# Hybrid encoder block on one core: attention's values behind the last forward output, a keys' piece and a queries' split at other places, the first output loads in one row

## The chip, the cores and the metric

The kernel runs on one core of a Trainium2 chip. The metric is the device time of one execution in microseconds (us), as the median of three runs; lower is better. A profiled execution is a separate one. The engines are TensorE (PE, with its weight loads PEld), VectorE (DVE), ScalarE (ACT), GpSimd (POOL) and SyncE (SP, which here issues DMAs only); ACT and POOL issue some DMAs too. Each engine works through its own instructions in a fixed order.

## What is computed

One layer of a bidirectional encoder with two branches, in float32:

```python
h = concat(meta_tokens, x)                       # 16 + 1024 = 1040 positions, D_MODEL = 1024
u = rms_norm(h) ; z = u @ w_in                   # one projection, split in ten parts:
rq, rk, rv, rg, aq, ak, av, ag, gr, ga = split(z)

# branch A: retention, 4 heads (dk 128, dv 256), chunks of 128, forward and backward
s     = (q k^T) * decay ;  inner = s v
state = chunk_decay * state + (k * k_decay)^T v        # scan over the chunks
o_r   = inner + (q * q_decay) state                    # both directions summed
y_r   = (group_norm(o_r) * ret_nw * silu(rg)) @ w_rb

# branch B: attention, 8 query heads, 2 key/value groups (hd 128), window +-128
aq, ak = rotary(aq), rotary(ak)
p   = softmax over [band of 3 x 128 keys | 16 meta keys | sink logit]
o_a = p[band] av + p[meta] av_meta
y_a = (o_a * silu(ag)) @ w_ab

mix = sigmoid(gr) * y_r + sigmoid(ga) * y_a
out = h + rms_norm(mix @ w_out, post_w)          # meta rows dropped
```

## The kernel before

**Precision and tiling.** Each fp32 product is made of three matmuls on upper and lower halves of the operands (`mm3`, L76 to L78). The upper half is a rounding cast on ACT or POOL, the lower half is value minus upper half on DVE (`dve_lo`, L92). So an operand is ready for PE only when ACT and then DVE are through with it. Tiles have 128 partitions; PSUM has eight banks, in four groups `pj` (3), `p1` (2), `p2` (2) and `p3` (1).

**Stages, in order of time.** Setup and retention of four heads; attention in 32 chunks of a head pair and 128 queries; then four phases of large projections, z (gates), r and a (the branches' projections) and o (the output). Each phase is a fast scheme of seven block products in place of eight: sums and differences of blocks of the left operand (tiles `st..S` such as sto1S, made on DVE at L1029) and of the right operand (T1 to T4, prepared early and fetched from DRAM by `get_pre`).

**Order.** A scheduler places the instructions of each engine by simulated times, within what the code demands: `follow(x)` and `tc.issue_after(x)` put what is issued inside behind instruction x on its engine. `latest` holds the last matmul, `last` named instructions, `marks` those of them that exist.

**Around the last head.** In retention `stage2` (L545) makes the forward output pa of a chunk in the one bank of `p3`: two `mm3`, then a scaled copy on ACT and an add on DVE (L557). Backward outputs pb_8 to pb_1 follow in a loop, each added on DVE (L645), transposed by PE (to, L621) and scaled on ACT (ost, L626). `gen_av` (L919) makes attention's values in nine pieces pav, the meta rows first; it is drawn from at three points behind the retention, the first without a condition, the second behind the last backward output.

**Attention.** For each chunk `stage1` makes scores ps, reduces them on DVE (L1467), takes exponentials on ACT (L1470), the reciprocal of their sum (L1474), and scales on POOL (L1483). `stage2` transposes p on PE (L1503 to L1508) and splits it in halves; `stage3` multiplies by the values (po). In between, `fill` draws projections of later queries and keys. The table `BEGUN` hooks work to steps of this fill: `keys(g, i)` splits the rotated keys of group g, piece i, in halves (kTh on ACT L742, kTl on DVE), `split_q(hp, e, i)` splits queries of head pair hp (aqh on ACT L695, aql on DVE). The rotation is two accumulating DMAs on POOL's queue (L192) behind two products on DVE (L187, L188).

**Loads of the phases.** `run` walks through all jobs (unit u, product p) and calls hooks at fixed steps. For phase o the raw blocks wro of units 0 and 1 are loaded 11 and 10 jobs before the phase (`o_load`, 512 KB each, from mx_d, which the branches have written); `refill("a", ...)` fetches T1 at -11 jobs, as a pair of transfers of 1 MB into both halves of big. u3a and u2a are sums in phase a, to which DVE adds a bank of PSUM (L1097); such a bank is free for PE's next product when it has been read.

Of the kernel before, what the change touches and what calls it, by code (L numbers as in the profile page):

```python
# [10 lines left out]
ALU = mybir.AluOpType  # L11
# [10 lines left out]
SCALE = 128 ** -0.5  # L22
# [17 lines left out]
def block_kernel(ctx: ExitStack, tc: tile.TileContext, x0, xT, x, meta, w_in, w_rb, w_ab, w_out, post_w,  # L40
# [50 lines left out]
    def dve_lo(o, i, hi):  # L91
        return nc.vector.tensor_tensor(o, i, hi.bitcast(F32), ALU.subtract).ins  # L92
# [377 lines left out]
    def retention(h, fill, begin=lambda: None):  # L470
# [11 lines left out]
        def qs(ts, c):  # L482
            return ts[(c - 1) // 4][:, P * ((c - 1) % 4):P * ((c - 1) % 4) + P]
# [64 lines left out]
        def stage2(c):  # L548
            n, vh, vl, kd, s = st1.pop(c)
            if c > 0:  # L550
                fh, fl = state["fs"]
                pa = p3(f"pa{h}_{c}")
                mm3(pa[:, 0:256], s[0], s[1], vh, vl, True, True)
                mm3(pa[:, 256:512], qs(qh, c), qs(ql, c), fh, fl, True, True)
                o = op[c - 1]
                nc.scalar.activation(o, pa[:, 0:256], AF.Copy, scale=rcol[:, c:c + 1])
                nc.vector.scalar_tensor_tensor(o, pa[:, 256:512], qdf(h, c), o, op0=ALU.mult, op1=ALU.add)  # L557
            if kd:
                pk = p2(f"pkv{h}_{c}")
            if "f" in kd:  # L560
                if c:
                    mm3(pk[:, 0:256], *kd["f"], vh, vl, True, True)
                else:
                    latest[:] = [nc.tensor.matmul(pk[:, 0:256], km, vm, start=True, stop=True).ins]
                new = rp.tile([P, 256], F32, tag="S", bufs=2, name=f"Sf{h}_{c}")
                if c == 0:
                    nc.vector.tensor_copy(new, pk[:, 0:256])
                else:
                    nc.vector.scalar_tensor_tensor(new, state["f"], cdf(h), pk[:, 0:256], op0=ALU.mult, op1=ALU.add)
                state["f"] = new  # L570
                state["fs"] = split_state(new, f"f{h}_{c}")
            if "b" in kd:
                a, b = kd["b"]
                mm3(pk[:, 256:512], a, b, vh, vl, True, True)
                nc.scalar.copy(kvb[c - 1], pk[:, 256:512])
# [154 lines left out]
    kT = {}  # L730
    wak = []

    rotated_k = {}

    def keys(g, i):

        if not i:
            kT[g] = [ra.tile([P, 4, 272], R, tag="kp", bufs=2, name=f"kT{s}{g}") for s in "hl"]
        kh, kl = kT[g]
        o = rotated_k.pop((g, i))  # L740
        s = NM if i == 0 else 0
        nc.scalar.copy(kh[:, i, 0:256], o[:, s:s + 256])  # L742
        dve_lo(kl[:, i, 0:256], o[:, s:s + 256], kh[:, i, 0:256])
        if i == 0:
            for j in range(4):
                nc.scalar.copy(kh[:, j, 256:272], o[:, 0:NM])
                dve_lo(kl[:, j, 256:272], o[:, 0:NM], kh[:, j, 256:272])
# [141 lines left out]
    def marks(*names):  # L889
        return [last[m] for m in names if m in last]  # L890
# [51 lines left out]


    av = gen_av()
    next(av)
    with follow(last["pb"]):
        next(av)
    with follow(*latest):
# [225 lines left out]
    def refill(nm, src):  # L1174
# [20 lines left out]
        def got(n):  # L1195
            return lambda: get_pre(n)

        def step(at, n, f):
            for k, j in enumerate(n):
                at.setdefault(j, []).append(lambda k=k: f(k))  # L1200
# [7 lines left out]
        if nm == "a":  # L1208
            at = {-16: [load(0, 0)], -14: [load(1, 1)]}
            each(at, -13, behind(split("B11", 0, 0)))  # L1210
            at.update({-11: [got("T1")], -10: [load(1, 0)], -9: [got("T2")], -5: [got("T3")], -1: [got("T4")]})
            each(at, -7, behind(split("B21", 1, 0)))
            each(at, -3, behind(split("B22", 1, 1)))
            return at
# [17 lines left out]
    def run(phases):  # L1232

        jobs = [(ph, u, p) for ph, _ in phases for u, p in ph.seq]
        hooks, i = {}, 0
        for ph, src in phases:
            i += len(ph.seq)
            if src:
                for j, f in refill(ph.nm, src).items():
                    hooks.setdefault(i + j, []).extend(f)  # L1240

        for u in (0, 1):
            hooks.setdefault(len(jobs) - len(ph_o.seq) - 11 + u, []).insert(0, lambda u=u: ph_o.block(u, "A11"))
        for k, at in enumerate((16, 27, 46, 58)):
            hooks[at] = [lambda k=k: pre_load(k, act_src(w_out))]
            for i in range(4):
                hooks[at + 4 + 2 * i] = [lambda k=k, i=i: pre_split(k, i, near[0])]
        n = 0
        for i, (ph, u, p) in enumerate(jobs):
            while n < min(i + LEAD, len(jobs)):  # L1250
                q, u_, p_ = jobs[n]
                q.prepare(u_, p_)
                n += 1
            yield
            ph.product(u, p)
            for f in hooks.get(i, ()):
                f()
# [83 lines left out]
        nc.vector.tensor_scalar(pw, pw, 0.5, None, op0=mul)  # L1341

    def o_load(t, u, j):
        nc.sync.dma_start(t, mx_d[4 * j:4 * j + 4, :, 256 * (u ^ 2):256 * (u ^ 2) + 256].rearrange("k p t -> p k t"))

    def o_post(u, i, j, o, to=None):
        if not rows:
# [82 lines left out]
    def attention():  # L1430
# [14 lines left out]
        def stage1(hp, n):  # L1445
# [10 lines left out]
            for x_ in range(2):  # L1456
# [7 lines left out]
                for c in ({0: (272, 336), 7: (208,)} if x_ else {0: (0,)}).get(n, ()):  # L1464
                    nc.vector.tensor_copy(r[:, c:c + 1], nsink[:, hp:hp + 1])
                o, w0 = (0, 64) if x_ else (1, 1)
                nc.vector.tensor_tensor_reduce(r[:, o:o + wid], s[:, 0:wid], seen, -SCALE,  # L1467
                                               nsink[:, hp:hp + 1], ALU.add, ALU.min, nm_[:, x_:x_ + 1])

                last["exp"] = nc.scalar.activation(pp[:, x_, w0 - o:w0 - o + 1 + wid], r[:, 0:1 + wid], AF.Exp,  # L1470
                                                   scale=-1.0, bias=nm_[:, x_:x_ + 1],
                                                   accum_out=den[:, x_:x_ + 1]).ins
                sides.append((wid, w0, blocks, moff))
            last["sum"] = nc.vector.reciprocal(den, den).ins  # L1474
            softmax.append(last["sum"])
            both = ap.tile([P, 2, 2, NM], F32, tag="pm2", bufs=2, name=f"pm2_{hp}_{n}")
# [86 lines left out]
        for k, (hp, n) in enumerate(chunks):  # L1563
# [15 lines left out]
            if not k:  # L1579
                with follow(*latest):  # L1580
                    fill(FILL[hp][n] - 5)
            with follow(*latest, *marks("exp", "sum")) if not ends else ExitStack():
                stage2(hp, n)
            if not ends:
# [7 lines left out]
            if k in (12, 14, 21):  # L1592
# [13 lines left out]
             76: [(sum_row, 3, 1)], 79: [(sum_fetch, 4)], 82: [(split_q, 2, 0, 0)], 88: [(sum_row, 4, 0)],  # L1606
             89: [(sum_row, 4, 1)], 90: [(split_q, 2, 1, 0)], 92: [(sum_fetch, 5)], 100: [(sum_row, 5, 0)],
             101: [(sum_row, 5, 1)], 102: [(fetch_aq, 3)], 104: [(keys, 1, 1)], 105: [(sum_fetch, 6)],
             110: [(split_q, 2, 0, 1)], 117: [(half_w, 'q', 3, 0)], 121: [(half_w, 'q', 3, 1)],
             122: [(pre_fetch, 9), (keys, 1, 2)], 123: [(sum_row, 6, 0)], 124: [(sum_row, 6, 1)], 126: [(split_q, 2, 1, 1)],  # L1610
             127: [(sum_fetch, 7)], 133: [(pre_sum, 9, 0)], 134: [(pre_sum, 9, 1)], 136: [(keys, 1, 3)],
             139: [(pre_sum, 9, 2)], 140: [(pre_parts, 9)], 141: [(pre_fetch, 10)], 145: [(split_q, 3, 0, 0)],
             146: [(sum_row, 7, 0)], 147: [(sum_row, 7, 1)], 150: [(split_q, 3, 1, 0)], 152: [(pre_sum, 10, 0)],
             153: [(pre_sum, 10, 1)], 155: [(pre_sum, 10, 2)], 157: [(pre_parts, 10)], 158: [(pre_fetch, 11)],
             164: [(split_q, 3, 0, 1)], 166: [(pre_sum, 11, 0)], 167: [(pre_sum, 11, 1)], 168: [(pre_sum, 11, 2)],
             170: [(pre_parts, 11)], 171: [(pre_fetch, 12), (split_q, 3, 1, 1)], 176: [(pre_sum, 12, 0)],
             178: [(pre_sum, 12, 1)], 179: [(pre_sum, 12, 2)], 181: [(pre_parts, 12)], 182: [(pre_fetch, 13)],
             187: [(pre_sum, 13, 0)], 188: [(pre_sum, 13, 1)], 189: [(pre_sum, 13, 2)], 190: [(pre_parts, 13)]}

# [112 lines left out]
```

## Time and profile before

| What | us |
|---|---|
| three runs | 1035.59, 1036.95, 1035.52 |
| their median | 1035.59 |
| profiled execution | 1040.78 |
| its span in the trace | 1039.0 |
| PE busy | 1023.5 |
| DVE busy | 834.6 |
| ACT busy | 505.2 |
| POOL busy | 230.1 |

Span is from the first to the last instruction of the trace. Rows of a timeline have the start in us from the span's start, the duration in us, engine, line, operation, output and inputs, shapes and count; in brackets the idle time of the engine just before, and what ended it. Matmuls overlap, so the next one starts before the listed duration is over. SPq, ACTq and POOLq are the sequencers that issue DMAs. The clock column is the granted clock of TensorE as a share of full speed.

### The profile page before, as it was taken

What the parts mean: (1) busy time and instruction counts of PE and PEld (TensorE: products, weight loads), DVE (VectorE), ACT (ScalarE), POOL (GpSimd) and SP (SyncE); (2) the same over time, 40 slices, a digit from 0 to 9 for tenths busy, and PEclk for the clock granted to TensorE, in tenths of its full rate; (3) what the DMA queues carried; (4) which work ended last, traced back from release to release, by engine and by line L of the source; (5) the groups of instructions that cost most, each with busy time, mean ns of one, the idle gap of its engine ahead of it and who ended that gap; (6) DMA issues with size and microseconds to landing.
All of it is one profiled execution on the core that took longest, in us unless ns stands there. A gap on an engine that the chain in (4) does not pass through costs nothing. (4 is left out here: it accounts for less than half of the span.)

```text
span 1039.0 us, 17320 instructions
## 1 busy us (share of the span) xinstructions
PE 1023.5 (99%) x5875; PEld 900.3 (87%) x5875; DVE 834.6 (80%) x1804; ACT 505.2 (49%) x1137; POOL 230.1 (22%) x368
## 2 busy tenths in 40 slices
PE   9999999999999999999999999999999999999997
PEld 8999999989998888988888888888888888887886
DVE  7787858769866778777769999998999899767765
ACT  5532332523423566655667555455567356243442
POOL 3445244243442323443310000000000000111042
PEclk9999999999999999999999999999999999999999
DMA  9433123242331457675559589898864846889463
GB/s 355 166 87 87 62 48 86 81 101 89 96 74 62 103 173 208 171 192 150 154 170 345 189 279 338 309 317 309 281 257 155 268 165 215 249 203 334 123 122 81
DMA packets 98840, 188.45 MB, mean 181 GB/s; under 512 B 13024, under 2 KB 37632, under 8 KB 98192
## 3 DMA queue, kind: packets, MB, share of 16 engines
q1 hardware_dynamic: 81200, 162.89, 46.4%
q0 software_dynamic: 10176, 14.73, 9.5%
q10 hardware_dynamic: 7376, 9.73, 2.8%
q8 instruction: 46, 0.75, 0.3%
q14 instruction: 42, 0.34, 0.1%
HBM read 124.32 MB, written 57.68 MB: 175 GB/s over the span
## 5 line engine op out<-in xcount | busy, mean ns | idle before, releaser
L1330 POOL DMA_DIRECT2D mx_d<-c1a x4 | 3.6, 892 | 395.1 <-DMA a<-in_w_out_dram 367.2
L77 PE MATMUL bz<-big,llz 128*128 128x512 f32 x192 | 74.8, 390 | 0.2 <-DVE llz L92 0.2
L78 PE MATMUL bz<-big,lhz 128*128 128x512 f32 x192 | 74.4, 389 | 0.0
L76 PE MATMUL bz<-big,lhz 128*128 128x512 f32 x192 | 74.1, 389 | 0.0
L76 PE MATMUL pv<-wh,big 128*128 128x256 f32 x256 | 72.9, 285 | 0.0
L78 PE MATMUL pv<-wl,big 128*128 128x256 f32 x256 | 72.6, 284 | 0.0
L77 PE MATMUL pv<-wh,big 128*128 128x256 f32 x256 | 72.2, 282 | 0.0
L77 PE MATMUL bz<-T,llz 128*128 128x512 f32 x176 | 68.5, 389 | 0.0
L78 PE MATMUL bz<-T,lhz 128*128 128x512 f32 x176 | 68.5, 389 | 0.0
L76 PE MATMUL bz<-T,lhz 128*128 128x512 f32 x176 | 68.1, 389 | 0.0
L1470 ACT ACTIVATE p<-raw,nm 128x337 f32<-128x337 f32 (+1 forms) x64 | 35.5, 556 | 36.5 <-DVE nm L1467 33.8
L1483 POOL TENSOR_SCALAR p<-p,den 128x336 f32<-128x336 f32 (+2 forms) x60 | 32.6, 566 | 87.9 <-DVE den L1474 87.8
L76 PE MATMUL paq<-big,wh 128*128 128x512 f32 x128 | 51.9, 406 | 0.0
L77 PE MATMUL paq<-big,wl 128*128 128x512 f32 x128 | 50.5, 394 | 0.0
L78 PE MATMUL paq<-big,wh 128*128 128x512 f32 x128 | 50.4, 394 | 0.0
L76 PEld LDWEIGHTS pv<-wh,big 128*128 128x128 f32 x256 | 48.4, 189 | 0.2
L77 PEld LDWEIGHTS pv<-wh,big 128*128 128x128 f32 x256 | 48.3, 189 | 0.0
L78 PEld LDWEIGHTS pv<-wl,big 128*128 128x128 f32 x256 | 48.2, 188 | 0.0
L77 PEld LDWEIGHTS bz<-big,llz 128*128 128x128 f32 x192 | 36.0, 188 | 8.0 <-DVE llz L92 0.5
L626 ACT ACTIVATE ost<-to,rnw 128x128 f32<-128x128 f32 x64 | 19.9, 366 | 46.6 <-PE to L621 36.2
L76 PEld LDWEIGHTS bz<-big,lhz 128*128 128x128 f32 x192 | 36.0, 188 | 7.4
L78 PEld LDWEIGHTS bz<-big,lhz 128*128 128x128 f32 x192 | 36.0, 188 | 7.4
(627 smaller groups left out, 3617.4 us busy)
## 6 DMA issues: line engine op xcount, KB each, us to landing
wrz<-in_w_in_dram SPq DMA_DIRECT2D x32, 512.0 KB, 5.8
wr<-in_w_in_dram SPq DMA_DIRECT2D x29, 512.0 KB, 3.8
we<-in_w_in_dram SPq DMA_DIRECT2D x16, 512.0 KB, 4.3
tg<-tg_d SPq DMA_DIRECT2D x32, 256.0 KB, 5.2
e<-e ACTq DMA_DIRECT2D x20, 256.0 KB, 2.8
e<-e SPq DMA_DIRECT2D x20, 256.0 KB, 4.7
xn<-in_x_dram SPq DMA_DIRECT2D x8, 512.0 KB, 9.3
oTr_d<-ost SPq DMA_DIRECT2D x16, 256.0 KB, 2.1
```

Source lines behind the costliest of these rows:

```text
L76: nc.tensor.matmul(o, ah, bh, start=first, stop=False, **kw)
L77: nc.tensor.matmul(o, al, bh, start=False, stop=False, **kw)
L78: latest[:] = [nc.tensor.matmul(o, ah, bl, start=False, stop=last, **kw).ins]
L626: nc.scalar.activation(ost[0][:, e_, w0:w0 + P], to[:, P * e_:P * e_ + P], AF.Copy, scale=rnw[:, 2 * h + e_:2 * h + e_ + 1])
L1330: nc.gpsimd.dma_start(d, to, accum_op=ALU.add)
L1470: last["exp"] = nc.scalar.activation(pp[:, x_, w0 - o:w0 - o + 1 + wid], r[:, 0:1 + wid], AF.Exp, scale=-1.0, bias=nm_[:, x_:x_ + 1], accu ...
L1483: nc.gpsimd.tensor_scalar(v, v, den[:, x_:x_ + 1], 1.0, op0=ALU.mult, op1=ALU.mult)
```

## The change

Four parts. Nothing is added or removed in the arithmetic; DMAs and matmuls are the same ones.

1. `stage2` notes the last matmul of pa. The first piece of the values begins only behind the last head's last pa.
2. `keys(1, 2)` is hooked at step 116 of the fill, before at 122. Its lower half is put aside and issued at the next `stage1`, right behind the second reduction of the scores.
3. `split_q(3, 1, 1)` leaves step 171 and stands just ahead of `stage2` of chunk (3, 2), behind the marks of the exponentials and the reciprocal.
4. Both first raw blocks of phase o are asked for at the same step, -11, and T1 is fetched behind the load asked for last (`asked`).

```diff
@@ retention, stage2
-                mm3(pa[:, 256:512], qs(qh, c), qs(ql, c), fh, fl, True, True)
+                last["pa"] = mm3(pa[:, 256:512], qs(qh, c), qs(ql, c), fh, fl, True, True)
...
@@ keys
-    rotated_k = {}
-
-    def keys(g, i):
+    rotated_k, lowers = {}, []
+
+    def keys(g, i, apart=False):
...
-        dve_lo(kl[:, i, 0:256], o[:, s:s + 256], kh[:, i, 0:256])
+        lower = lambda: dve_lo(kl[:, i, 0:256], o[:, s:s + 256], kh[:, i, 0:256])
+        if apart:
+            lowers.append(lower)
+        else:
+            lower()
...
@@ behind the retention
     av = gen_av()
-    next(av)
+    with follow(last["pa"]):
+        next(av)
     with follow(last["pb"]):
         next(av)
...
@@ refill
+        def got_behind(n):
+            def f():
+                with follow(*asked):
+                    get_pre(n)
+            return f
...
-            at.update({-11: [got("T1")], -10: [load(1, 0)], -9: [got("T2")], -5: [got("T3")], -1: [got("T4")]})
+            at.update({-11: [got_behind("T1")], -10: [load(1, 0)], -9: [got("T2")], -5: [got("T3")], -1: [got("T4")]})
...
@@ run
         for u in (0, 1):
-            hooks.setdefault(len(jobs) - len(ph_o.seq) - 11 + u, []).insert(0, lambda u=u: ph_o.block(u, "A11"))
+            hooks.setdefault(len(jobs) - len(ph_o.seq) - 11, []).insert(u, lambda u=u: ph_o.block(u, "A11"))
...
     def o_load(t, u, j):
-        nc.sync.dma_start(t, mx_d[4 * j:4 * j + 4, :, 256 * (u ^ 2):256 * (u ^ 2) + 256].rearrange("k p t -> p k t"))
+        asked[:] = [nc.sync.dma_start(
+            t, mx_d[4 * j:4 * j + 4, :, 256 * (u ^ 2):256 * (u ^ 2) + 256].rearrange("k p t -> p k t")).ins]
...
@@ attention, stage1
-                nc.vector.tensor_tensor_reduce(r[:, o:o + wid], s[:, 0:wid], seen, -SCALE,
-                                               nsink[:, hp:hp + 1], ALU.add, ALU.min, nm_[:, x_:x_ + 1])
+                scored = nc.vector.tensor_tensor_reduce(r[:, o:o + wid], s[:, 0:wid], seen, -SCALE,
+                                                        nsink[:, hp:hp + 1], ALU.add, ALU.min, nm_[:, x_:x_ + 1]).ins
...
+            with tc.issue_after(scored):
+                while lowers:
+                    lowers.pop(0)()
             last["sum"] = nc.vector.reciprocal(den, den).ins
...
@@ attention, the loop over chunks
+            if chunks[k] == (3, 2):
+                with follow(*marks("exp", "sum")):
+                    split_q(3, 1, 1)
             with follow(*latest, *marks("exp", "sum")) if not ends else ExitStack():
                 stage2(hp, n)
...
@@ BEGUN
-             110: [(split_q, 2, 0, 1)], 117: [(half_w, 'q', 3, 0)], 121: [(half_w, 'q', 3, 1)],
-             122: [(pre_fetch, 9), (keys, 1, 2)], 123: [(sum_row, 6, 0)], 124: [(sum_row, 6, 1)], 126: [(split_q, 2, 1, 1)],
+             110: [(split_q, 2, 0, 1)], 116: [(keys, 1, 2, True)], 117: [(half_w, 'q', 3, 0)], 121: [(half_w, 'q', 3, 1)],
+             122: [(pre_fetch, 9)], 123: [(sum_row, 6, 0)], 124: [(sum_row, 6, 1)], 126: [(split_q, 2, 1, 1)],
...
-             170: [(pre_parts, 11)], 171: [(pre_fetch, 12), (split_q, 3, 1, 1)], 176: [(pre_sum, 12, 0)],
+             170: [(pre_parts, 11)], 171: [(pre_fetch, 12)], 176: [(pre_sum, 12, 0)],
```

What this moves, in the order of the instructions. First SP, ahead of phase o (wro_0 of unit 0 and of unit 1, a: the last part of B22, big: the T1 pair, T_7786: the first half of T2). Before:

```order
L1344 DMA wro_0_11297<-mx_d 128x4x256
L1266 DMA a_11333<-in_w_out_dram 128x512
L1162 DMA big_112<-preT_96 128x4x512
L1162 DMA big_113<-preT_97 128x4x512
L1344 DMA wro_0_11325<-mx_d 128x4x256
L1162 DMA T_7786<-preT_98 128x2048
```

and now:

```order
L1355 DMA wro_0_11297<-mx_d 128x4x256
L1277 DMA a_11333<-in_w_out_dram 128x512
L1355 DMA wro_0_11299<-mx_d 128x4x256
L1167 DMA big_112<-preT_96 128x4x512
L1167 DMA big_113<-preT_97 128x4x512
L1167 DMA T_7786<-preT_98 128x2048
```

The second wro load has moved ahead of the T1 pair. On DVE, behind the first of these loads (lla_3: lower halves for products of phase a; c1a: a sum of phase a), before:

```order
L1029 TENSOR_TENSOR sto0S_11483<-wro_0_11297 128x512
L92 TENSOR_TENSOR lla_3_11340<-sta2S,lha_3_11339 128x512
L92 TENSOR_TENSOR lla_3_11364<-sta3S,lha_3_11363 128x512
L1097 TENSOR_TENSOR c1a_11216<-c1a_11216,ba_2_11367 128x512
L1029 TENSOR_TENSOR sto1S_11509<-wro_0_11325 128x512
```

and now:

```order
L1034 TENSOR_TENSOR sto0S_11483<-wro_0_11297 128x512
L92 TENSOR_TENSOR lla_3_11340<-sta2S,lha_3_11339 128x512
L1034 TENSOR_TENSOR sto1S_11509<-wro_0_11299 128x512
L92 TENSOR_TENSOR lla_3_11364<-sta3S,lha_3_11363 128x512
L1102 TENSOR_TENSOR c1a_11216<-c1a_11216,ba_2_11367 128x512
```

sto1S has moved ahead of one lower half and of c1a.

ACT at the keys' piece (wh: upper halves of weights; oa, oTa_d: output of a chunk; p: exponentials; pah, pm, pbh: halves of transposed p). Before:

```order
L118 CAST wh_0_6433<-wr_0_6258 128x1024
L1543 COPY oa_6_6384<-po_7_6453 128x2x128
L1546 DMA oTa_d<-oa_6_6384 128x2x256
L1470 ACTIVATE p_4891,den_2_6464<-raw_0_6307,nm_2_6463 128x337
L1470 ACTIVATE p_4891,den_2_6464<-raw_1_6315,nm_2_6463 128x337
L1513 CAST pah_1_6492<-pt_2_1_6483 128x512
L1516 CAST pm_4885<-pt_2_1_6488 32x128 x2
L1523 CAST pbh_1_6497<-pt_2_1_6488 128x256
L118 CAST wh_1_6507<-wr_1_6259 128x1024
L742 CAST kTh_6208<-akr_2_6360 128x256
```

and now:

```order
L118 CAST wh_0_6434<-wr_0_6258 128x1024
L742 CAST kTh_6208<-akr_2_6360 128x256
L1558 COPY oa_6_6384<-po_7_6454 128x2x128
L1561 DMA oTa_d<-oa_6_6384 128x2x256
L1482 ACTIVATE p_4891,den_2_6465<-raw_0_6307,nm_2_6464 128x337
L1482 ACTIVATE p_4891,den_2_6465<-raw_1_6315,nm_2_6464 128x337
L1528 CAST pah_1_6494<-pt_2_1_6485 128x512
L1531 CAST pm_4885<-pt_2_1_6490 32x128 x2
L1538 CAST pbh_1_6499<-pt_2_1_6490 128x256
L118 CAST wh_1_6509<-wr_1_6259 128x1024
```

kTh, before behind wh_1, now stands behind wh_0, ahead of the oa copy and its DMA. Its lower half on DVE, before:

```order
L1467 ISA nm_2_6463 128x1
L1474 RECIPROCAL den_2_6464<-den_2_6464 128x2
L92 TENSOR_TENSOR pal_1_6493<-pt_2_1_6483,pah_1_6492 128x512
L92 TENSOR_TENSOR pm_4885<-pt_2_1_6488,pm_4885 32x128 x2
L92 TENSOR_TENSOR pbl_1_6498<-pt_2_1_6488,pbh_1_6497 128x256
L92 TENSOR_TENSOR wl_1_6508<-wr_1_6259,wh_1_6507 128x1024
L92 TENSOR_TENSOR kTl_6209<-akr_2_6360,kTh_6208 128x256
```

and now:

```order
L1479 ISA nm_2_6464 128x1
L92 TENSOR_TENSOR kTl_6209<-akr_2_6360,kTh_6208 128x256
L1489 RECIPROCAL den_2_6465<-den_2_6465 128x2
L92 TENSOR_TENSOR pal_1_6495<-pt_2_1_6485,pah_1_6494 128x512
L92 TENSOR_TENSOR pm_4885<-pt_2_1_6490,pm_4885 32x128 x2
L92 TENSOR_TENSOR pbl_1_6500<-pt_2_1_6490,pbh_1_6499 128x256
L92 TENSOR_TENSOR wl_1_6510<-wr_1_6259,wh_1_6509 128x1024
```

kTl has moved ahead of the reciprocal and everything that stood between.

PE at the last head's tail (pb: backward outputs, to: transposes, pav: values). Before:

```order
L76 MATMUL pb_2_4567<-Shb_3_4507,qh_0_3647 128x256
L77 MATMUL pb_2_4567<-Shb_3_4507,ql_0_3648 128x256
L78 MATMUL pb_2_4567<-Slb_3_4508,qh_0_3647 128x256
L621 MATMUL to_4_4580<-ident,op_3_3642 128x128 x2
L76 MATMUL pb_1_4586<-Shb_2_4563,qh_0_3647 128x256
L77 MATMUL pb_1_4586<-Shb_2_4563,ql_0_3648 128x256
L78 MATMUL pb_1_4586<-Slb_2_4564,qh_0_3647 128x256
```

and now:

```order
L76 MATMUL pb_2_4567<-Shb_3_4507,qh_0_3647 128x256
L77 MATMUL pb_2_4567<-Shb_3_4507,ql_0_3648 128x256
L78 MATMUL pb_2_4567<-Slb_3_4508,qh_0_3647 128x256
L77 MATMUL pav_4785<-wh_1_4619,big_113 128x256
L78 MATMUL pav_4785<-wl_1_4620,big_112 128x256
L76 MATMUL pav_4785<-wh_1_4619,big_112 128x256
L77 MATMUL pav_4785<-wh_1_4619,big_113 128x256
L78 MATMUL pav_4785<-wl_1_4620,big_112 128x256
L76 MATMUL pav_4785<-wh_1_4619,big_112 128x256
L77 MATMUL pav_4785<-wh_1_4619,big_113 128x256
L78 MATMUL pav_4785<-wl_1_4620,big_112 128x256
L621 MATMUL to_4_4580<-ident,op_3_3642 128x128 x2
```

pb_2, before directly ahead of to_4, now has eight matmuls of the values behind it.

## The prediction

> **What bounds the kernel now.** I read the page's busy shares first, then PE's list of waits, then the clock by windows, and last the timelines around the waits that the diff touches.
>
> ```profile
> span 1039.0 us, 17320 instructions
> PE 1023.5 (99%) x5875; PEld 900.3 (87%) x5875; DVE 834.6 (80%) x1804; ACT 505.2 (49%) x1137; POOL 230.1 (22%) x368
> ```
>
> TensorE (PE) is busy for 1023.5 of 1039.0 us and executes the same instructions after the change as before. So the time can move in two ways only: by PE's waits, and by the clock at which PE works. The waits, with the sum in us, the number and the longest:
>
> ```profile
> PE ba L76 <- DVE u3a L1097: 1.8, 1, 1.8
> ...
> PE ps L76 <- ACT kTh L742: 1.1, 1, 1.1
> PE pe L77 <- DVE wel L92: 1.0, 2, 0.6
> ...
> PE pb L76 <- DVE op L645: 0.4, 1, 0.4
> PE ps L78 <- DVE kTl L92: 0.4, 1, 0.4
> ```
>
> The clock, in windows of 3.4 us behind a wait of 0.65 us at 326.88 (for ACT's ost, untouched by the change) and behind the two largest of the list, and in a dense stretch (PE's busy time and count come first behind the length; then the other engines, the granted clock, DMA):
>
> ```profile
> 326.90:330.30 3.40, 3.40 (x28) 3.36 (x29) 2.59 (x13) 2.30 (x7) 0.00 (x0) 1.00 0.60 193
> ...
> 458.60:462.00 3.40, 3.40 (x15) 3.08 (x14) 3.40 (x12) 2.25 (x8) 0.10 (x1) 0.50 0.75 232
> 946.70:950.10 3.40, 3.40 (x10) 2.62 (x9) 3.40 (x8) 0.00 (x0) 0.00 (x0) 0.50 1.00 326
> 560.00:700.00 140.00, 140.00 (x620) 115.91 (x619) 131.70 (x218) 74.34 (x131) 0.00 (x0) 1.00 0.85 292
> ```
>
> At full clock a 512-wide matmul takes 140.00 / 620 = 0.226 us. Behind the keys' waits (1.1 + 0.4) and behind the 1.8 us wait the granted clock is 0.50 for 3.4 us, which costs 3.4 / 2 = 1.7 us each. Behind the 0.65 us it is 1.00. Each of the diff's four parts points at one or two of these waits.
>
> **The first output loads.** SP issues, the landing of the first wro load, of the second, and of the T1 pair between them (min, median, max):
>
> ```profile
> 925.83 0.38 SPq L1344 DMA_DIRECT2D wro<-mx_d  x1
> 926.30 0.46 SPq L1266 DMA_DIRECT2D a<-in_w_out_dram  x1
> 926.85 1.28 SPq L1162 DMA_DIRECT2D big<-preT  x2
> 928.22 0.59 SPq L1344 DMA_DIRECT2D wro<-mx_d  x1
> ...
> DMA to landing us min/median/max: 3.5/3.5/3.5
> ...
> DMA to landing us min/median/max: 10.8/10.8/10.8
> ...
> DMA to landing us min/median/max: 8.0/9.0/10.0
> ```
>
> The first load lands 3.5 us after its issue; the second, behind two transfers of 1 MB, needs 10.8 and lands at 939.0. On VectorE (DVE) everything is queued behind the first operation that reads it, sto1S; then the rows of ACT and PE:
>
> ```profile
> 939.11 0.69 DVE L1029 TENSOR_TENSOR sto1S<-wro 128x512 f32<-128x512 f32 x1 [5.46 <-DMA wro<-mx_d]
> ...
> 945.13 0.68 DVE L1097 TENSOR_TENSOR u3a<-u3a,ba 128x512 f32<-128x512 f32 x1
> ...
> 938.40 0.59 ACT L1094 COPY u3a<-ba 128x512 f32<-128x512 f32 x1 [1.80 <-PE ba L78]
> ...
> 943.64 0.39 PE L76 MATMUL bo<-big,lho 128*128 128x512 f32 x1
> 945.87 0.50 PE L76 MATMUL ba<-big,lha 128*128 128x512 f32 x1 [1.83 <-DVE u3a L1097]
> ...
> 950.31 0.39 PE L76 MATMUL ba<-T,lha 128*128 128x512 f32 x1
> ```
>
> DVE stood idle for 5.46 us, then worked from 939.11 to 945.81 without a pause until u3a had been read out of its bank; PE wanted that bank at 943.64 + 0.23 = 943.87. In the changed order the second load is issued where the T1 pair was, at about 926.85, behind one wro load and one small one. With the first load's 3.5 us it lands at 930.4, with 1.2 us more for the company at 931.6. u3a then depends on ACT's copy alone (938.99), so it ends near 940, 4 us before PE asks. The twelve matmuls from 945.87 to 950.31 would stand from 943.87 to 943.87 + 12 x 0.226 = 946.6: **gain 3.7** (2.0 of wait and restart, 1.7 of clock). Bounds: the slow landing can stay. If it takes L us from 926.85, PE's stall is 926.85 + L + 6.7 (the DVE work behind sto1S) + 1.2 (a lower half and c1a, 0.6 each, now also behind sto1S) - 943.87, which is nothing up to L = 9.1 and 1.7 at L = 10.8. So the gain is 3.7 for L from 3.5 to 9.1, and about 0.3 at the slow end; I take 3.7, since what the 10.8 was queued behind is no longer ahead. What is late instead: the T1 pair, by one issue of 0.6 us and 0.5 MB of transfer, some 1.5 us. It lands by 926.85 + 10.0 + 1.5 = 938.4, and at 950.31 PE still works on the phase before the one that reads it.
>
> **The keys' piece.** ACT, the rotation's issue on POOL, its landing, and DVE's place for the lower half:
>
> ```profile
> 451.12 0.37 ACT L1543 COPY oa<-po 128x256 f32<-128x256 f32 x1 [1.25 <-PE po L1538]
> ...
> 455.43 1.05 ACT L118 CAST wh<-wr 128x1024 fp32r<-128x1024 f32 x1
> 456.38 0.41 ACT L742 CAST kTh<-akr 128x256 fp32r<-128x256 f32 x1
> ...
> 443.33 1.69 POOL L192 DMA_DIRECT2D akr<-m_ak  x2 [0.58 <-DVE akr L188]
> ...
> DMA to landing us min/median/max: 8.1/8.1/8.1
> ...
> 453.34 0.08 DVE L1467 DVE_READ_ACCUMULATOR2_ANT nm<- 128x1 f32 x1
> 454.29 0.17 DVE L1474 RECIPROCAL den<-den 128x2 f32<-128x2 f32 x1 [0.87 <-ACT p L1470]
> ```
>
> Now kTh is cast behind a 1.05 us weight cast and read at once; PE waits 1.1 us for it and 0.4 for kTl. In the changed order kTh stands one weight cast earlier, ahead of the oa copy at 451.12, where ACT idles for 1.25 us. It can't start before the rotation has landed, 443.33 + 8.1 = 451.4 for the first half and some 0.6 later for the second, so near 452.0; it ends at 452.4, and the oa copy and the two exponentials behind it on ACT run 0.1 to 0.6 us late. kTl (0.42) falls into DVE's 0.87 us of idle ahead of the reciprocal. Both are ready 2 us before PE wants them at 455.7. Removed: 1.13 + 0.41 of wait (the 1.1 and 0.4 above), 1.7 of clock: 3.25. What is late next is the chunk's softmax, since PE comes 3.25 us sooner to
>
> ```profile
> 463.03 1.67 POOL L1483 TENSOR_SCALAR p<-p,den 128x336 f32<-128x336 f32 x2
> ...
> 466.83 0.27 PE L1503 MATMUL pt<-ident,p 128*128 128x128 f32 x1
> ```
>
> POOL's scaled p ends at 464.7 and the transposes are wanted at 466.83 - 3.25 = 463.6. The exponentials feeding POOL also come sooner, but behind rotation issues on POOL and a DVE that is nearly full; I put back 0.5 us (0.3 to 1.1, the latter with POOL not a moment sooner). **Gain 2.75**; bounds 0 (the wait only moves) and 3.25.
>
> **The queries' split (3,1,1).** The upper half on ACT, the lower half on DVE, the weights' lower half behind it:
>
> ```profile
> 511.11 0.62 ACT L695 CAST aqh<-aq 128x512 fp32r<-128x512 f32 x1
> ...
> 512.79 0.69 DVE L92 TENSOR_TENSOR aql<-aq,aqh 128x512 fp32r<-128x512 f32 x1
> ...
> 515.19 1.23 DVE L92 TENSOR_TENSOR wel<-we,weh 128x1024 fp32r<-128x1024 f32 x1
> ...
> 518.35 0.31 PE L77 MATMUL ps<-kTh,aql 128*128 128x336 f32 x1
> ```
>
> The split moves behind the chunk's exponentials and reciprocal, so aqh's 0.62 leaves ACT ahead of weh and aql's 0.69 leaves DVE ahead of wel. wel ends some 0.6 us earlier, and one of the two wel waits (0.41) goes: **gain 0.45** with PE's restart. aql then ends at about 517.3, before its first reader at 518.35 less 0.45; if it were later, the gain would be lost (bounds -0.3 and 0.6). The other wel wait, 0.6, stays.
>
> **The last head's tail.** PE's first matmul of pa_8, the DVE operation that frees its bank, and the wait further on:
>
> ```profile
> 301.43 0.28 PE L76 MATMUL pa<-vh,sh 128*128 128x256 f32 x1
> ...
> 298.66 0.48 DVE L557 SCALAR_TENSOR_TENSOR op<-pa,qd,op 128x256 f32<-128x256 f32 x1
> ...
> 322.48 0.36 PE L76 MATMUL pb<-Shb,qh 128*128 128x256 f32 x1 [0.45 <-DVE op L645]
> ```
>
> pa_8 goes ahead of 17 of the values' matmuls, some 0.115 us each, to 301.43 - 2.0 = 299.5; its bank is free at 299.14. Further on, pb_2 had nothing between itself and pb_1 but a transpose pair, so pb_1 waited 0.45 us for DVE; now eight of the values' matmuls (0.9 us) stand between. **Gain 0.4**, bounds -0.2 (pa_8's bank read later than 299.14) and 0.5.
>
> **Sum.** 3.7 + 2.75 + 0.45 + 0.4 = 7.3 us off the span of 1039.0, of which 3.4 is the two half-clock stretches; the waits alone are 3.9. The profiled execution took 1040.78 us, its span and 1.8 around it, 5.2 more than the median of 1035.59. The three runs differ by 1.4 (1035.52 to 1036.95), nearly one stretch of 1.7, so a usual run holds fewer of them than the profiled one. I count 3.9 + 1.2 = 5.1 for the median: **1030.5 us**. For the profiled execution I expect 1040.8 - 7.3 = 1033.5.
>
> On the clock, the Trainium skill ("TensorE: Matmul & The Clock Gate", Part 1) describes a free-running window of 3413 ns with half or full rate, where an idle window brings half rate. The windows above agree with the length and the rate, but here 1.5 and 1.8 us of waiting were followed by it, not 3.4.
>
> **Rivals.** *The clock's stretches come anyway*, at a phase that these waits don't set. Against it: two stretches in the trace, each right behind one of the two largest waits. For it: the runs' unequal times. Gain 3.9, the waits alone, so 1031.7. That is the result by the rule of the Trainium skill's page named above, since neither wait fills a window.
>
> *The keys' wait only moves*: the rotation's landing (8.1 us) is what ACT now waits for, so each us more holds the exponentials of that chunk, and POOL's scaling holds PE at the transposes for as long as kTh did. For it: POOL's 464.7 against 463.6. Against it: only 1.1 us of that is exposed at worst. Gain 7.3 - 2.75 = 4.55 in the trace, about 3.3 in the median: 1032.3.
>
> *The second load stays slow*, since the mx_d it reads or the T1 pair right behind it holds it, not its place in the queue. For it: 10.8 us, and a DMA share of 1.00 soon after (946.70 above). Against it: the first load's 3.5. Gain 0.3 + 3.6 in the trace, about 2.2 in the median: 1033.4. This covers the case that the change doesn't do there what it says.
>
> *Slower*: the second load becomes later than before, at one place. With 7.9 us of DVE work now between sto1S and u3a's end, PE's stall outgrows the old 2.0 plus the 3.6 won elsewhere from L = 926.85 + L + 7.9 - 943.87 = 5.6, thus L above 14.8; each further us costs one. At L = 17.5 the time is 1038.3. For it: the T1 pair competes and ACT, PE and DVE all hang on one queue. Against it: no landing quoted here is above 10.8.
>
> **How the numbers follow.** Chances: forecast 0.56, the clock's own phase 0.14, keys' wait moved 0.10, slow load 0.11, slower 0.09. The likeliest case alone spans 1028.3 (all 7.3 in the median too) to 1031.7. For 8 in 10 the range takes in the keys' and the load's rival, and below the forecast the runs that lose a stretch each: **1027.3 to 1034.2 us**. A measurement here tells 0.2% (2.1 us) from no change, so faster means below 1033.5. Faster 0.82 (the forecast, the clock's rival, most of the keys' one and a third of the slow load), same 0.11 (the rest of these and the mildest of the last), slower 0.07.
>
> **What would show it.** Right: the second wro load lands within 5 us; DVE's 5.46 us of idle ahead of sto1S is gone; PE's list has no ba wait for u3a, no ps wait for kTh or kTl, no pb wait for op and one wel wait instead of two; the clock shows no 0.50 window between PE's first matmuls and the end; ACT idles some 2 us ahead of kTh for the DMA of akr; a small new wait stands at the transposes near 463. Wrong: a sto1S that still waits for its DMA beyond 936, a pt wait above 1 us, or 0.50 windows at places where no wait stands.

## The result and the profile after

The changed kernel takes 1032.66 us in the median of seven runs (1031.61 to 1034.67), the kernel before, on the same chips, 1037.18 us (1035.52 to 1038.33). The ratio is 0.9962, with a 95% interval from 0.995 to 0.9975: 3.9 us faster, between 2.6 and 5.2. The forecast was 1030.5 (1027.3 to 1034.2) and 5.1 us. The profiled executions lie further apart: a span of 1029.8 us after, 1039.0 before, so 9.2 us, where the trace's sum had promised 7.3. The profiled execution after is the fastest of its seven runs, that of before, 1040.78, was slower than all seven of its kernel. Most of what follows is on that gap between 9.2 and 3.9: the first profiled execution lies 3.6 us above the median of before, that of the changed kernel 1.1 below its own.

The head of the page after:

```profile
span 1029.8 us, 17323 instructions
PE 1019.0 (99%) x5875; PEld 898.1 (87%) x5875; DVE 834.9 (81%) x1804; ACT 505.3 (49%) x1137; POOL 228.2 (22%) x368
```

PE's list of waits after (sum, number, longest), from the second row on:

```profile
PE pq L76 <- ACT big L342: 0.8, 2, 0.4
PE to L621 <- ACT ost L626: 0.6, 1, 0.6
PE to L621 <- DVE sd L534: 0.3, 1, 0.3
PE pk L77 <- DVE wl L92: 0.2, 1, 0.2
PE pt L1518 <- POOL p L1498: 0.2, 1, 0.2
```

All waits that the diff pointed at are gone: u3a, kTh, kTl, op, and both of wel. One new one has come, 0.2 us at the transposes for POOL's p, at 462.96. There is no window at half clock before PE's last matmul; the two stretches of the chunk and of the phase, with columns as in the prediction's windows:

```profile
453.00:460.00 7.00, 7.00 (x47) 6.45 (x46) 6.02 (x18) 6.88 (x19) 2.25 (x6) 1.00 0.67 184
936.00:943.00 7.00, 7.00 (x33) 5.79 (x31) 5.30 (x11) 2.73 (x6) 0.00 (x0) 1.00 1.06 371
```

The first output loads after, on SP, then the landing of the second load, DVE's rows behind it, and PE where it waited before:

```profile
918.98 0.37 SPq L1355 DMA_DIRECT2D wro<-mx_d  x1
919.44 0.46 SPq L1277 DMA_DIRECT2D a<-in_w_out_dram  x1
919.99 0.39 SPq L1355 DMA_DIRECT2D wro<-mx_d  x1
920.46 1.29 SPq L1167 DMA_DIRECT2D big<-preT  x2
...
DMA to landing us min/median/max: 6.2/6.2/6.2
...
926.25 0.69 DVE L1034 TENSOR_TENSOR sto1S<-wro 128x512 f32<-128x512 f32 x1 [2.31 <-DMA wro<-mx_d]
...
933.69 0.69 DVE L1102 TENSOR_TENSOR u3a<-u3a,ba 128x512 f32<-128x512 f32 x1
...
938.24 0.39 PE L76 MATMUL bo<-big,lho 128*128 128x512 f32 x1
938.46 0.39 PE L76 MATMUL ba<-big,lha 128*128 128x512 f32 x1
```

The second load is issued 1.0 us behind the first and lands 6.2 us after its issue, in place of 10.8. u3a has been read at 934.38; PE asks for the bank at 938.46 and gets it at once, 4.1 us after that. At the keys ACT waits for the rotation (akr), and kTl fills DVE's idle time, as laid out in the prediction:

```profile
449.97 0.41 ACT L742 CAST kTh<-akr 128x256 fp32r<-128x256 f32 x1 [0.76 <-DMA akr<-m_ak]
...
452.68 0.42 DVE L92 TENSOR_TENSOR kTl<-akr,kTh 128x256 fp32r<-128x256 f32 x1
453.63 0.17 DVE L1489 RECIPROCAL den<-den 128x2 f32<-128x2 f32 x1 [0.53 <-ACT p L1482]
...
454.79 0.32 PE L76 MATMUL ps<-kTh,aqh 128*128 128x336 f32 x1
```

Set instruction against instruction on PE, the time between the two traces grows by 0.6 us at the head's tail, 3.3 at the keys (3.6 there, less 0.3 at the next transposes), 0.5 at the first wel, 0.85 at the second, 3.7 at the loads; 0.2 are spread.

### The profile page after: what moved, and what is told of

The parts are those of the page before. It is cut to its first block, busy times and chain, and to the rows that moved or that the text cites. A ratio compares the mean times of both kernels' runs of the same rounds, so it can differ in the third digit from the quotient of the medians.

```text
span 1029.8 us, 17323 instructions
## 1 busy us (share of the span) xinstructions
PE 1019.0 (99%) x5875; PEld 898.1 (87%) x5875; DVE 834.9 (81%) x1804; ACT 505.3 (49%) x1137; POOL 228.2 (22%) x368
## 5 line engine op out<-in xcount | busy, mean ns | idle before, releaser
L556 ACT ACTIVATE op<-pa,rcol 128x256 f32<-128x256 f32 x32 | 15.2, 475 | 53.8 <-PE pa L78 52.9
```

## The experiments

In all runs the kernel before was timed on the same chip; differences in us are worked out from the ratio, with its 95% interval.

### The parts alone

**Part 4 alone** is these lines put into the kernel before, and nothing else of the diff:

```diff
+                with follow(*asked):
+                    get_pre(n)
...
+            hooks.setdefault(len(jobs) - len(ph_o.seq) - 11, []).insert(u, lambda u=u: ph_o.block(u, "A11"))
```

> The kernel before with part 4 alone (both first output loads in one row, T1 behind them). My theory: the second load's late landing alone made PE wait 1.8 us for u3a, and the half-clock stretch behind it comes from that wait. In the trace the ba wait for u3a and the 0.50 window near 947 are gone, the keys' wait and its 0.50 window near 460 stay; between the times of the two kernels 2.0 us (waits alone) to 3.7 us are won. Rival (the clock's stretches come at a phase that waits don't set): 2.0 us are won and a 0.50 window may stand anywhere. Rival (T1, T2 or T3 become late in exchange): a new wait in phase o, under 1 us won.

Measured: ratio 0.9986 (0.9973 to 0.9999), 1.4 us faster (0.1 to 2.8). The trace has no u3a wait; the keys' waits (1.19 and 0.41) and the half-clock window behind them stand as before. So the order does what it should. The gain lies under the 2.0 us expected for the waits alone, though the interval holds that.

**Part 2 alone** is this, with `lowers` emptied behind the second score reduction:

```diff
+             110: [(split_q, 2, 0, 1)], 116: [(keys, 1, 2, True)], 117: [(half_w, 'q', 3, 0)], 121: [(half_w, 'q', 3, 1)],
+             122: [(pre_fetch, 9)],
```

> The kernel before with part 2 alone (keys 1,2 earlier, its lower half behind the next score reduction). My theory: the ps waits for kTh and kTl (1.1 and 0.4 us) and the 0.50 window near 460 go, a wait of at most 0.5 us for POOL's p comes in, and 1.3 us (waits alone) to 3.3 us are won; the u3a wait and its 0.50 window near 945 stay. Rival (the wait only moves to the transposes): a pt wait above 1 us and under 0.5 us won.

Measured: ratio 0.9985 (0.9975 to 0.9995), 1.6 us faster (0.5 to 2.6). kTh and kTl are gone from the waits, the transposes wait 0.23 us for POOL. And although nothing was changed at the loads, PE waited there hardly at all:

```profile
PE ba L76 <- DVE u3a L1101: 0.2, 1, 0.2
```

**Parts 1 and 3 alone:**

```diff
+    with follow(last["pa"]):
+        next(av)
...
+            if chunks[k] == (3, 2):
+                with follow(*marks("exp", "sum")):
+                    split_q(3, 1, 1)
```

> The kernel before with parts 1 and 3 alone. My theory: the pb wait for op (0.45) goes by part 1, and part 3 takes both wel waits (0.4 and 0.6 to 0.8), since the second one hangs on a raw weight buffer that the first wel frees. In the trace none of these three waits is left above 0.3 us; 1.0 to 1.9 us are won. Rival (prediction as written, the second wel wait stays): one wel wait of 0.6 us or more is left and about 0.9 us are won. The u3a and kTh waits are as before and vary.

Measured: ratio 0.9994 (0.9984 to 1.0003), 0.6 us faster with no change inside the interval. The op wait and the first wel wait are gone; of the second wel wait 0.38 us are left, between my theory and its rival.

**The full change without part 4**, so with the lines of the first experiment left as in the kernel before:

> The changed kernel with part 4 undone (parts 1 to 3 alone). My theory: the second load's wait for u3a is set by how late the last written sums of mx_d land, from 0 to 1.8 us over executions, so part 4 is worth 1 to 1.5 us in the mean and this kernel is 2.3 to 3 us faster than before, against 3.8 for the full change. Rival (the 1.8 us wait and its half-clock stretch come in most executions): part 4 is worth 3.7 us and this kernel is about 0.5 us faster than before or equal to it.

Measured: ratio 0.9982 (0.9972 to 0.9991), 1.9 us faster (0.9 to 2.9), a little under what I expected; the rival's 0.5 us lies outside the interval. Against the 3.9 us of the full change, part 4 is worth about 2 us behind the others, some 1.6 more or less by the two intervals. The trace has a u3a wait of 0.65 us. The three groups alone add up to 1.4 + 1.6 + 0.6 = 3.6, near the 3.9 of all together; an interaction smaller than the intervals, 1 to 1.3 us each way, would not show.

### Both kernels once more

> The kernel before, unchanged, to see how much of its first trace repeats. My theory: the waits for u3a, kTh, kTl, wel and op repeat within 0.3 us in every execution, since the order is fixed, while the half-clock stretches behind the two large ones come in some executions only; the time is 1035.5 to 1039 and, where both stretches show, 1039 or more. Rival (each large wait brings its stretch every time): two 0.50 windows of 3.4 us in this trace too.

The time is the same as before's (0.9997, 0.9987 to 1.0008), but this profiled execution took 1035.08 us, where the first took 1040.78. Its waits:

```profile
PE pe L77 <- DVE wel L92: 0.8, 1, 0.8
PE ps L76 <- ACT kTh L742: 0.7, 1, 0.7
...
PE pb L76 <- DVE op L645: 0.5, 1, 0.5
PE ps L78 <- DVE kTl L92: 0.4, 1, 0.4
```

No u3a wait at all, 0.7 in place of 1.1 for kTh, and no half-clock window. My theory had the waits the same in every execution: that was wrong. With PE's instructions set against those of the first trace, 2.0 of the 5.7 us between the two lie at the keys, 0.6 at the first wel and 3.6 at the loads; 0.7 go the other way between the wel waits and the loads.

> The changed kernel, unchanged, to see why its runs spread from 1031.6 to 1034.7 with a mean clock of 0.998 to 0.999 in each. My theory: the difference between such runs is in DMA landings at the kernel's start or in the phases, seen as PE waits for a DMA-fed operation that the first trace doesn't have; no 0.50 window. Rival (half-clock stretches in some runs): a 0.50 window of 3.4 us with 1.7 us more time.

Ratio 0.9964 (0.9952 to 0.9977), 3.7 us faster, as in the first measurement. No half-clock window, so the rival falls for this execution; but the 1.8 us that it is longer than the first of its kernel don't come from DMA at the start either. They come between 456 and 523 us, mainly in steps of 0.4, 0.3, 0.3 and 0.7: the first is a wait of 0.27 us at the transposes for pbl with PE's restart behind it, the last one of 0.52 for the second wel; at the two in between no wait above 0.15 us stands in the trace.

### What the u3a wait hangs on

The first wro load is issued 0.1 us after an accumulating write of phase a (POOL's, u2a into mx_d) has landed: 925.71 and 925.83 in the first trace. In five executions with the old order of the loads (times in us; u3a read is worked out as the start of sto1S plus the 6.7 us of DVE work):

| trace | write issued | lands after | first load issued | sto1S starts | + 6.7: u3a read | PE asks | wait |
|---|---|---|---|---|---|---|---|
| before | 916.34 | 9.37 | 925.83 | 939.11 | 945.81 | 943.87 | 1.83 |
| part 2 alone | 913.01 | 8.09 | 921.21 | 934.11 | 940.81 | 940.54 | 0.17 |
| before again | 914.42 | 7.61 | 922.14 | 934.83 | 941.53 | 941.95 | none |
| parts 1 and 3 | 915.47 | 7.64 | 923.23 | 936.38 | 943.08 | 943.00 | none |
| without part 4 | 912.99 | 8.13 | 921.24 | 934.58 | 941.28 | 940.52 | 0.65 |

The way from the issue to the reading of u3a has nearly one length, 19.4 to 20.0 us. What differs is how long before PE's request the load is issued: 18.0 us in the first trace, 19.3 to 19.8 in the others. And nearly all of that is the landing of the write: in each of the five PE asks 27.53 us behind the write's issue (in the five traces with the new order and no late write too, within 0.01). The write and its landing, in the first trace:

```profile
916.34 0.86 POOL L1330 DMA_DIRECT2D mx_d<-u2a  x1 [0.35 <-DVE u2a L1321]
...
DMA to landing us min/median/max: 9.4/9.4/9.4
```

and in before's second execution:

```profile
914.42 0.86 POOL L1330 DMA_DIRECT2D mx_d<-u2a  x1 [0.36 <-DVE u2a L1321]
...
DMA to landing us min/median/max: 7.6/7.6/7.6
```

Why one landing takes longer than another stays open. To test the dependence, six GpSimd operations on an idle table were put ahead of the writes, in both kernels:

```diff
+                if (u, i, j) == (1, 0, 1):
+                    with follow(*written):
+                        idle = [nc.gpsimd.tensor_scalar(rbc[:, 0:512], rbc[:, 0:512], 1.0, 1.0, op0=mul,
+                                                        op1=mul).ins for _ in range(6)]
+                with follow(*idle):
+                    written[:] = [nc.gpsimd.dma_start(d, to, accum_op=ALU.add).ins]
```

> The kernel before, with six GpSimd operations of 128x512 on a table that is idle there (times one, so nothing changes in it) ahead of the last-but-two accumulating write of mx_d, the landing of which releases the first output load on SP. They put that write some 3.3 us later. My theory: the u3a wait of PE is how late this write lands, less a slack; in the old order that slack is used up (waits of 0 to 1.8 us in five executions), so the wait becomes 3 to 5 us, with one half-clock stretch or two behind it, and the kernel is 3.5 to 7 us slower than before. Rival (the wait comes from the 10.8 us of transfers and not from when they begin): wait at most 1.8 us, under 1.5 us slower.

Measured: ratio 1.0037 (1.0014 to 1.0059), 3.8 us slower than before (1.5 to 6.1). POOL, DVE and the wait in this trace:

```profile
912.04 6.04 POOL L1333 TENSOR_SCALAR rbc<-rbc 128x512 f32<-128x512 f32 x6
918.03 0.88 POOL L1336 DMA_DIRECT2D mx_d<-c5a  x1
918.60 1.20 POOL L1336 DMA_DIRECT2D mx_d<-u2a  x1
...
938.95 0.69 DVE L1029 TENSOR_TENSOR sto1S<-wro 128x512 f32<-128x512 f32 x1 [5.00 <-DMA wro<-mx_d]
...
945.70 0.50 PE L76 MATMUL ba<-big,lha 128*128 128x512 f32 x1 [2.35 <-DVE u3a L1097]
```

The load now goes out 15.9 us ahead of PE's request. The wait is 2.35 us and not 3 to 5, since the second load took only 8.9 us this time and the write is 2.9 us late against PE, not 3.3; 938.95 + 6.7 - 943.19 = 2.46 fits the table. The half-clock stretch that I expected behind it did not come in this trace, and this execution, 1038.99 us, is only 1.8 us above the median of before: the trace accounts for a part of the 3.8. The six operations also hold up the load of their table, issued at 805.83 before and on SP at 918.11 here, where SP waits 3.9 us for them; what that costs was not separated.

> The changed kernel with the same six operations. My theory: part 4 brings the second load in some 5 us sooner, and u3a is ready about 4 us before PE asks (934.4 against 938.5 in the trace after), so the 3.3 us are covered: no u3a wait above 0.5 us, and the kernel is within 1 us of the changed one, 3 to 4 us faster than before. Rival (part 4 only shifts the wait to T1 or T2, which are now behind two loads): a new PE wait in phase o or a u3a wait of 2 us or more, and no more than 1.5 us faster than before.

Measured: ratio 0.9976 (0.9964 to 0.9988), 2.5 us faster than before (1.2 to 3.7), 1.4 us behind the 3.9 of the full change and a little less than I expected. With the load only 15.4 us ahead of the request, sto1S starts at 931.99 (the second load goes out 2.8 us behind the first here and lands 3.4 us after its issue), u3a has been read at 939.89, and PE asks at 941.10: no wait. So part 4 doesn't remove a fixed stall. It makes a slack of 3.7 to 4.1 us (five traces; 1.2 with the late write) where there was one of -1.9 to 0.4, and it pays as much as the write lands late in an execution.

### When the clock goes to half

Waits of eight sizes were put into phase z of the changed kernel. GpSimd writes blocks 1 and 2 of a left operand again, with the values that they have, between the matmuls of block 1 and those of block 2:

```diff
+    SPOTS = {16: 1, 26: 2, 36: 3, 46: 4, 56: 5, 66: 2, 76: 3, 86: 4}
...
+                    if k == 2:
+                        for _ in range(n):
+                            pool_hi(h[:, 1:3], h[:, 1:3].bitcast(F32))
```

> The changed kernel with waits of eight sizes put into phase z: at eight products, 27 us apart, GpSimd writes two of the four blocks of the left operand's upper half again (same values) 1, 2, 3, 4, 5, 2, 3 and 4 times between the second and the third block's matmuls, so that PE waits some 0.5 us for each time. My theory: the clock goes by a grid of windows of 3.41 us, counted from the first full-clock window; a window in which PE is busy for less than some share between 0.55 and 0.78 is followed by one at 0.50, wherever the wait comes from. So waits up to 0.75 us have no effect beyond themselves, those above 1.5 us cost 1.7 us more when they fall in one window and may cost nothing more when they are divided between two. Rival (the size of the wait alone decides): all waits above one size are followed by a 0.50 window, whatever the grid. Rival (only a window wholly idle lowers the clock): none of these waits, all under 3.4 us, has any such effect.

> The same kernel as in the run before, for a second position of the grid against the waits. My theory: the waits have the same sizes within 0.1 us; those of 1.0 to 2.0 us may change sides, by the busy share of the windows that they fall in. Rival (size alone decides): the same waits are followed by 0.50 windows as in the first execution.

Measured: 1072.15 and 1066.93 us, one execution each. Each writing cost PE some 0.9 us in the mean, not the 0.5 that I had reckoned with. The records of the granted clock show a grid: every full-clock stretch of every trace is a whole number of 3.413 us windows long (in the first trace of before 133, then one at half, 142, one at half, 25). The first such stretch begins 4.3 to 7.4 us into the span, at another place in each execution, so the grid doesn't start with the kernel. Of the same wait (three writes) the first execution shows this, in windows on that grid:

```profile
645.72:649.13 3.41, 1.93 (x9) 1.27 (x7) 3.41 (x6) 1.70 (x3) 1.23 (x3) 1.00 1.05 410
649.13:652.54 3.41, 3.01 (x13) 2.52 (x14) 3.41 (x7) 1.25 (x2) 0.34 (x1) 1.00 0.93 335
```

and the second this:

```profile
643.42:646.83 3.41, 1.32 (x7) 1.05 (x7) 3.41 (x6) 0.77 (x2) 1.79 (x3) 1.00 1.01 390
646.83:650.24 3.41, 3.41 (x10) 2.67 (x9) 3.41 (x7) 1.66 (x3) 0.00 (x0) 0.50 0.76 242
```

PE waited 1.88 us in the one and 2.09 in the other. In the first the wait is divided: PE is busy for 1.93 / 3.41 = 0.57 and 0.88 of the two windows, and the clock stays. In the second it lies in one window with a share of 0.39, and the next one runs at 0.50. The waits of 4.2 and 6.0 us brought two such windows each time, that of 3.1 us in one execution of two. Half of the waits had the same size in both executions (1.54, 2.15, 4.2 and 6.0 us), but not all: the one of two writes at the second place was 2.93 us in the first and absent in the second, where PE had other work in between.

The share of a window is the part of it in which PE is busy. Over all twelve traces, leaving out the kernel's end and windows that are at half clock themselves: after a share of 0.46 or less the next window was at half clock each time (11 windows), from 0.48 to 0.55 three times in six, from 0.57 on never, so the limit lies lower than the 0.55 to 0.78 that I expected; what decides between 0.48 and 0.55 stays open. So the size of a wait alone doesn't decide (the 2.35 us of the late write, with a share of 0.52, left the clock as it was; the 1.83 us of before, with 0.46, did not), and a wholly idle window isn't needed: both rivals fall. For the keys' waits before, 1.13 + 0.41, 1.19 + 0.41 and 1.32 + 0.41 us were followed by a half-clock window (shares 0.55, 0.53, 0.49), 0.71 + 0.41, divided between two windows, and 0.63 + 0.41 were not (0.79 and 0.81):

```profile
453.06:456.47 3.41, 2.70 (x24) 2.50 (x23) 2.21 (x6) 3.39 (x11) 2.33 (x6) 1.00 0.86 226
456.47:459.89 3.42, 3.01 (x20) 2.60 (x21) 3.32 (x8) 2.63 (x6) 0.00 (x0) 1.00 0.47 125
```

These are the two windows of before's second execution.

How often this happens in timed runs can be read from their mean clock, which is on record for each. A trace with no half-clock window ahead of PE's last matmul has 0.998 or 0.999, one with one such window 0.997, the first trace of before with its two 0.995. Of 100 timed runs with the keys in their old place (before, part 4 alone, parts 1 and 3) 21 have 0.997 or less; of 46 with the keys moved, 23 of them with the old order of the loads, none has. So the stretch at the keys comes in about one run of five, and the one at the loads hardly ever.

## Why the prediction was right, and where it was off

**The loads.** The mechanism was right: place in the queue, sto1S, the DVE work behind it, u3a, the bank. The price in the trace was right to the tenth (3.7). What was wrong is that it was taken for every execution: "I take 3.7". The wait was 1.83 us in the trace that was to be read, and 0 to 0.65 in four others; one of the five had the half-clock window. Their mean is 0.53 us of wait and 0.2 windows, under 1 us, and by the mean clocks of the timed runs the window is rarer still; measured were 1.4 alone and about 2 behind the other parts. The intervals reach down to 0.1 and 0.4, so this fits, but whether the loads are worth 0.5 us or 2 stays open. The second load's landing was off, and luckily without a price: it took 6.2 us (5.3 to 6.6 in the five traces without the late write) where 3.5 to 4.7 were counted on and under 5 was the sign of being right, and DVE still idles 2.31 us for it. The prediction's own bound, no loss up to 9.1, covers that. That a usual run holds fewer half-clock stretches was seen and counted; that the wait itself is a matter of the execution was not.

**The keys.** Predicted 2.75, in the trace 3.3: put back were 0.23 us at the transposes in place of 0.5. In the timed runs it is 1.6 (0.5 to 2.6). Over five executions with the keys in their old place the waits are 1.0 to 1.7 us, 1.4 in the mean. The half-clock window comes in three of these five but in about a fifth of the timed runs, so 1.4 + 0.2 x 1.7 - 0.23 = 1.5 would be expected, close to the 1.6 measured. ACT idles 0.76 us for the rotation, where some 2 were a sign of being right; kTh is in time all the same.

**The split.** The first wel wait went, as said (0.5 against 0.45), but it too is a draw: of five traces with the old split it stands in three (0.41 to 0.54 us) and is missing in two. "The other wel wait, 0.6, stays" was wrong: it went in the first trace, which gave 0.85 us, and shrank from 0.61 to 0.77 (0.74 in the mean of five traces) to 0.22 to 0.55 in six others with part 3. The traces show why, before:

```profile
516.44 0.33 SPq L819 DMA_DIRECT2D we<-in_w_in_dram  x1
516.47 0.50 PE L77 MATMUL pe<-big,wel 128*128 128x512 f32 x1 [0.41 <-DVE wel L92]
520.01 0.69 DVE L831 TENSOR_TENSOR we<-we,we 128x512 f32<-128x512 f32 x1 [1.39 <-DMA we<-in_w_in_dram]
527.28 1.22 DVE L92 TENSOR_TENSOR wel<-we,weh 128x1024 fp32r<-128x1024 f32 x1 [0.63 <-ACT weh L841]
528.56 0.50 PE L77 MATMUL pe<-big,wel 128*128 128x512 f32 x1 [0.61 <-DVE wel L92]
```

and after:

```profile
509.74 1.23 DVE L92 TENSOR_TENSOR wel<-we,weh 128x1024 fp32r<-128x1024 f32 x1
521.85 1.23 DVE L92 TENSOR_TENSOR wel<-we,weh 128x1024 fp32r<-128x1024 f32 x1
523.13 0.50 PE L77 MATMUL pe<-big,wel 128*128 128x512 f32 x1
```

The end of the first wel frees the raw tile (516.42 before), the next load of raw weights is issued at once (516.44), lands at 519.99, DVE's operation on it starts at 520.01, with the score reductions queued behind, and the second wel follows; from the end of the first wel to the start of the second it takes 10.9 us before and after (10.9 to 11.4 in all twelve traces). When the first came 0.87 us earlier against PE, the second did too. A wait of the same kind further along one chain is not a separate one.

**The tail.** 0.4 predicted for op, 0.45 gone; the 0.64 us for ost stayed, as said.

**The sum.** 7.3 for the trace, 9.2 found: 0.85 for the second wel, 0.55 at the keys, 0.4 at the tail and in between. For the median 5.1, measured 3.9 (2.6 to 5.2). The discount from trace to median (7.3 to 5.1) was of the right kind, for only part of the reason: 1.2 of the 3.4 us of half clock were counted, some 0.7 stretches a run, where the mean clocks show about 0.2, and the u3a wait was counted whole. The second wel wait, left out of the sum, made up for a part of that. From the means over the traces I estimate 0.5 for the loads, 1.5 for the keys, 0.7 for both wel waits and 0.45 for the tail, 3.2 in sum, inside the interval. That 1032.66 lies 2.2 us above the forecast is for the most part the base: the three runs it started from have a median of 1035.59, all seven 1037.18.

The rivals: in gain, the clock's own phase (3.9) is closer to what was measured than the forecast, and the interval holds both, so the time doesn't decide between them; the traces do. That rival is half right: the grid is free of the kernel, but what happens in a window decides, and the stretches go when the waits go. Its 3.9 is met by luck, since it counts the u3a wait of 1.83 us whole. That the keys' wait only moves is refuted by 0.23 us at the transposes. The second load did not stay slow (6.2 us against 10.8), nor did it become slower: it took 3.4 to 6.6 us in the six traces with the new order.

## What to carry to other kernels

A wait of 1 to 2 us behind a DMA in one profiled execution is one draw: compute the slack from issue to need, take a second trace, and count the mean of the wait, not the one that was seen. The mean clock of each timed run then says how often a half-clock stretch comes. A wait that takes TensorE below about half of a 3.4 us window cost 1.7 us more here, so one large wait is dearer than the same time in several places. And before a wait is called untouched, follow the buffer that the removed one freed: here the next load hung on it.

## What was not expected of the hardware

The clock's windows lie on a grid of 3.413 us, and the half rate follows a window with TensorE busy for less than about half of it (0.46 and less always, 0.57 and more never), where 1.5 us of waiting can be enough and 2.35 us, divided between two windows, can be too little. The rule of the Trainium skill ("TensorE: Matmul & The Clock Gate", Part 1), half rate after an idle window, fits the grid and the rate; the idle window it asks for was not needed in these traces.

The loads of 512 KB ahead of phase o took 3.4 to 3.9 us from their issue where nothing large was right ahead of them, 5.3 to 6.6 about a microsecond behind another of their size, and 8.9 to 10.9 behind 2 MB.
